# A hybrid state-space and attention network in fp32 on one core: the turned state-space steps listed anew, piece by piece, and the squares added on VectorE

## The chip, the cores and the metric

One core of a Trainium2 chip. The metric is device time in microseconds of one execution of the whole program (256 tokens through 4 layers). Shown are the median of three runs and, for the profile, one execution taken by the hardware profiler.

## The reference

Four layers of width 1024 on 256 tokens. Each layer is a half-weighted SwiGLU feed-forward (hidden width 2816), a mixer, and a second half-weighted feed-forward, each followed by a residual sum and a layer norm. The mixers are a Mamba-2 state-space mixer (layers 0 and 3), a forgetting attention (layer 1) and a block attention (layer 2). The change concerns the state-space mixer:

```python
zxbcdt = x @ w_in                                   # z 2048, x 2048, b 512, c 512, dt 32
xbc = silu(causal_conv4(xbc) + conv_b)
dt = softplus(dt + dt_bias); a = -exp(a_log)
decay = exp(segsum(dt * a))                         # per head, 256 x 256, lower triangle
y = ((c @ b.T) * decay) @ (x * dt) + x * d_skip     # 4 groups of 8 heads of 64
y = y * silu(z)
y = y * rsqrt(mean(y**2 over the 512 of a group) + eps) * norm_w
out = y @ w_out
```

## The kernel before, in words

All products run on TensorE (PE) in float32r, with each operand split in a high and a low part: `mm3` (L183) and `proj_T` (L269) issue three matmuls for one product. ACT makes the high part of a weight piece (`wh`, L156), DVE the low part (`wl`, L157). Weights stream from memory as pieces of 128x2048 fp32, 1 MB each, fetched by the SP queue (`fetch`, L159) two pieces ahead of use, with 3 raw and 5 split buffers.

The 256 tokens are two halves, t = 0 and t = 1, each a Python generator that takes one piece per step; the driver (L930 to L945) runs t = 1 two pieces behind t = 0. A state-space stage has 29 pieces in the order of `SSM_ORDER` (L44): X0 (4 pieces, not turned), Z0 (2, not turned), and then X1 to X3 (3 each), Z1 to Z3 (2 each) and the output pieces O0 to O3 (2 each), where the digit is the group. For X and Z of groups 1 to 3 the product is made once for both halves, turned (channels on the partitions), within t = 1; t = 0 has no work in these pieces. O pieces are done by each half for itself.

After a piece's product a list `post` names the steps that are issued: `at(i, step, ...)` appends a step to piece i. The steps of a group g are:

- `stage_T` (L493): ACT copies the turned product out of PSUM (L497), then the causal convolution (`conv`, L451: ACT L457, DVE L461) and its Silu (L464).
- `stage_e` (L531): the SP queue loads a row of cumulative sums broadcast over partitions, ACT makes four Relu (L544) and one Exp (L545), and for i = 1 one more Exp (L542). Tiles "mt", 5 buffers.
- `stage_back` (L502): three matmuls of b and c (L514), eight transposes (L521), DVE scales (L509, L524, L526).
- `stage_m` (L547) and `stage_y` (L552): DVE applies c b to the decays, PE makes y into a "gu" PSUM tile, DVE adds the skip (L570) into the tile Y.
- `stage_z` (L573): ACT's Silu of z (L575). `stage_g` (L577): DVE multiplies Y by it (L583, L589), ACT squares it (L592), POOL adds the squares of the two tiles (L593) and then the two halves of that (L594).
- `stage_r` (L597): PE sums over partitions with a column of ones (L601), DVE L603, POOL takes the power -1/2 (L605). `stage_n` (L607): PE broadcasts (L610), DVE scales Y (L615). `stage_a` (L617): Y is split into high and low parts for the O pieces.

PSUM has 8 banks: two each of "acc0" and "acc1", "gu" and "tp". Before the first output piece (less two) the turned products use the acc tiles, after that the "gu" tiles, since the output accumulators need all four (L679). The transposes and y use "tp" and "gu".

The list gives the program order. A scheduler then orders each engine's instructions by their readiness, with the program order as priority; `keep_in_program_order` pins an instruction behind what its engine was given before it (the matmuls of back and y are pinned).

Of the kernel before, what the change touches and what calls it, by code (L numbers as in the profile page):

```python
# [7 lines left out]
F32 = mybir.dt.float32  # L8
# [8 lines left out]
S = 256  # L17
# [9 lines left out]
N_GRP = 4  # L27
# [6 lines left out]
PF = 2  # L34
WB = 5
RB = 3

# [41 lines left out]
def build(tc, x, wst, ln_g, ln_b, sm_rows, sm_conv, fx_b, out, plan=None):  # L79
# [318 lines left out]
    def ssm_small(j):  # L398
        if j in ssms:
            return ssms[j]  # L400
        consts()
        s = St()
        s.rows = tmp(64, "rows", 1)
        tc.keep_in_program_order(nc.sync.dma_start(s.rows, bc(sm_rows[j:j + 1, :], 64)))
        s.conv = spool.tile([128, 24, 7], F32, name="conv", bufs=1)
        nc.sync.dma_start(s.conv, sm_conv[j])
        s.na = tmp(32, "na", 1)
        tc.keep_in_program_order(nc.scalar.activation(s.na, s.rows[:, 32:64], AF.Exp))
        nc.vector.tensor_scalar_mul(s.na, s.na, -1.0)
        s.xb, s.cv, s.xs, s.th, s.Y, s.cb, s.mt, s.d = {}, {}, {}, {}, {}, {}, {}, {}  # L410
        s.ahs = [{}, {}]
        ssms[j] = s
        return s

    def ssm(st, j):
# [77 lines left out]
        def stage_T(g, n):  # L493

            if n == 0:
                frame(g)
            nc.scalar.activation(s.xb[g][:, 2 * n:2 * n + 2, 3:3 + S],  # L497
                                 bank.pop(("X", g, n)).rearrange("p (a b) -> p a b", a=2), AF.Copy)
            if n:
                conv(g, 0 if n == 1 else 4, 2 * n + 2)  # L500

# [29 lines left out]
        def stage_e(g, qd, i):  # L531

            def tile_e():
                return spool.tile([128, 4, 128], F32, name="mt", bufs=5)
            e = tile_e()
            h0 = g * 8 + qd * 4
            row = s.d[i].cum[h0:h0 + 4, :].rearrange("h l -> (h l)").unsqueeze(0)
            nc.sync.dma_start(e.rearrange("p a b -> p (a b)"), row.to_broadcast([128, 512]))
            s.mt[g, qd, i] = e
            if i == 1:  # L540
                o = s.mt[g, qd, 2] = tile_e()
                nc.scalar.activation(o, e, AF.Exp)  # L542
            for h in range(4):
                nc.scalar.activation(e[:, h], e[:, h], AF.Relu, scale=-1.0, bias=s.d[i].cums[:, h0 + h:h0 + h + 1])  # L544
            nc.scalar.activation(e, e, AF.Exp, scale=-1.0)  # L545
# [25 lines left out]
                                               op0=ALU.mult, op1=ALU.add)  # L571

        def stage_z(g, n):  # L573
            th = s.th[g, n] = tmp(512, "nw" if g else "xD", 2)
            nc.scalar.activation(th, bank.pop(("Z", g, n)), AF.Silu)  # L575

        def stage_g(g):  # L577

            for n in range(2):
                Y = s.Y[g, n]  # L580
                if g:
                    th = s.th.pop((g, n)).rearrange("p (a b) -> p a b", a=2)
                    nc.vector.tensor_mul(Y, Y, th)  # L583
                else:
                    th = s.th.pop((0, n))
                    tp = transposes(th, 4).rearrange("p (n a b) -> p n a b", n=2, a=2)
                    for k in range(2):
                        Yk = s.Y[0, k][:, :, tok[n]]
                        nc.vector.tensor_mul(Yk, Yk, tp[:, k])  # L589
            sq = [tmp(512, "nw", 2) for n in range(2)]  # L590
            for n in range(2):
                nc.scalar.activation(sq[n], s.Y[g, n].rearrange("p a b -> p (a b)"), AF.Square)  # L592
            nc.gpsimd.tensor_add(sq[0], sq[0], sq[1])  # L593
            nc.gpsimd.tensor_add(sq[0][:, 0:S], sq[0][:, 0:S], sq[0][:, S:2 * S])  # L594
            s.sq = sq[0]

        def stage_r():  # L597

            ps = T()
            for i in range(2):  # L600
                nc.tensor.matmul(ps[:, i:i + 1], s.sq[:, tok[i]], K["cut"][:, 128:129], start=True, stop=True)  # L601
            ss = s.ss = small()
            nc.vector.tensor_scalar(ss[:, 0:2], ps[:, 0:2], 1.0 / 512, EPS, op0=ALU.mult, op1=ALU.add)  # L603
            for i in range(2):
                nc.gpsimd.tensor_tensor(ss[:, 2 + i:3 + i], ss[:, i:i + 1], mhalf, op=ALU.pow)  # L605

        def stage_n(g):  # L607
            ps = T()
            for i in range(2):
                nc.tensor.matmul(ps[:, tok[i]], s.ss[:, 2 + i:3 + i].to_broadcast([128, 128]), ident, start=True, stop=True)  # L610
            for n in range(2):
                for i in range(2):
                    w = s.conv[:, g * 6 + 2 * n + i]
# [22 lines left out]
        if t == 0:  # L636
            at(where["Z", 0, 1], stage_z, 0, 0)
        else:
            at(where["Z", 0, 1], stage_z, 0, 1)
# [24 lines left out]
        first_o = where["O", 0, 0]  # L664
        for i, (kind, g, n) in enumerate(pieces):
            if kind == "X" and g == 0:
                if n % 2 == 0:
                    ps = bank["b" if n == 0 else 0] = GA(int(n == 0))
            elif kind == "Z" and g == n == 0:
                ps = bank["Z", 0, t] = GA(1)  # L670
            w = yield
            if kind == "O":
                down(st, *s.ahs[t][g][n], w, g == 0 and n == 0, g == 3 and n == 1)
# [2 lines left out]
            elif kind == "Z" and g == 0:  # L676
                proj512(st, ps, n, w)
            elif t == 1:
                ps = bank[kind, g, n] = GA(int(kind == "Z")) if i < first_o - LAG else G()  # L679
                proj_T(ps, w)  # L680
            for f, a in post.get(i, ()):
                f(*a)
# [14 lines left out]
    def attn(st, kind, j):  # L697
# [62 lines left out]
        def stage_s(g):  # L760
# [18 lines left out]
            pt = [tmp(512, "mt", 5) for b in range(1 + t)]  # L779
# [21 lines left out]
        def att(g):  # L801

            pT = ps_.pop(g) if away(g) else []
            for p in () if away(g) else ps_.pop(g):
                tp = transposes(p, 4)
                e = tmp(512, "mt", 5)
                if t == 0:
                    nc.vector.tensor_copy(e, tp)
                else:
# [266 lines left out]
```

## Time and profile before

| | us |
|---|---|
| median of 3 runs (lowest, highest) | 2111.68 (2108.36, 2114.94) |
| the profiled execution, its own time | 2111.97 |
| its span, first to last instruction | 2110.1 |
| busy in the span: PE / weight loads / DVE / ACT / POOL | 2077.8 / 1759.7 / 1462.3 / 1169.3 / 527.4 |

The first state-space stage lies at about 193 to 385 us of the span, the second at about 1721 to 1913 us. PE is the matmul engine, PEld its weight loads, which run beside matmuls. A matmul is drawn longer than the distance to the next one, since matmuls are pipelined. "Idle before" with an arrow names what ended the wait.

### The profile page before, as it was taken

What the parts mean: (1) busy time and instruction counts of PE and PEld (TensorE: products, weight loads), DVE (VectorE), ACT (ScalarE), POOL (GpSimd) and SP (SyncE); (2) the same over time, 40 slices, a digit from 0 to 9 for tenths busy, and PEclk for the clock granted to TensorE, in tenths of its full rate; (3) what the DMA queues carried; (4) which work ended last, traced back from release to release, by engine and by line L of the source; (5) the groups of instructions that cost most, each with busy time, mean ns of one, the idle gap of its engine ahead of it and who ended that gap; (6) DMA issues with size and microseconds to landing.
All of it is one profiled execution on the core that took longest, in us unless ns stands there. A gap on an engine that the chain in (4) does not pass through costs nothing.

```text
span 2110.1 us, 31413 instructions
## 1 busy us (share of the span) xinstructions
PE 2077.8 (98%) x11034; PEld 1759.7 (83%) x11034; DVE 1462.3 (69%) x2912; ACT 1169.3 (55%) x2409; POOL 527.4 (25%) x937
## 2 busy tenths in 40 slices
PE   8999999999999999999999999999999999999998
PEld 7888988888888889788888889788888889888886
DVE  6557988765665676765675676755575589888565
ACT  6445998444544454545454455544545459984442
POOL 2331001233133313043233302033233310012331
PEclk9999999999999999999999999999999999999999
DMA  9766544677586665477676666376666765446762
GB/s 318 224 230 214 194 165 155 222 232 230 177 273 218 226 224 188 149 237 230 203 241 228 225 222 200 135 242 229 224 227 228 226 214 185 165 155 230 228 226 94
DMA packets 228493, 444.98 MB, mean 211 GB/s; under 512 B 21168, under 2 KB 21744, under 8 KB 228336
## 3 DMA queue, kind: packets, MB, share of 16 engines
q1 hardware_dynamic: 197616, 395.65, 55.4%
q0 software_dynamic: 30720, 47.34, 7.9%
q8 instruction: 86, 1.41, 0.3%
q14 instruction: 71, 0.58, 0.1%
HBM read 418.15 MB, written 24.76 MB: 210 GB/s over the span
## 4 chain that ended last, share of the span: by engine, by line
PE 87%; DVE 6%; ACT 4%; DMA 2%; issue 1%; POOL 0%; DVEq 0%; ACTq 0%; POOLq 0%
PE gu L184 15%; PE gu L187 15%; PE gu L188 15%; PE acc L184 9%; PE acc L187 9%; PE acc L188 9%; PE ga L276 2%; PE ga L278 2%; PE ga L277 2%; DVE wl L157 2%; PE tp L196 2%; ACT wh L156 1%; PE ga L184 1%; DVE cv L461 1%; PE ga L188 1%; PE ga L187 1%
## 5 line engine op out<-in xcount | busy, mean ns | idle before, releaser
L157 DVE TENSOR_TENSOR wl<-raw,wh 128x512 fp32r<-128x512 f32 (+1 forms) x1412 | 891.0, 682 | 348.0 <-ACT wh L156 346.5
L156 ACT ACTIVATE wh<-raw 128x512 fp32r<-128x512 f32 (+1 forms) x1412 | 779.3, 620 | 548.0 <-PE gu L188 217.0
L184 PE MATMUL gu<-wh,x 128*128 128x512 f32 x1408 | 548.8, 390 | 1.9 <-ACT wh L156 1.2
L188 PE MATMUL gu<-wh,x 128*128 128x512 f32 x1408 | 549.1, 390 | 0.0
L187 PE MATMUL gu<-wl,x 128*128 128x512 f32 x1408 | 548.8, 390 | 0.0
L300 POOL DMA_DIRECT2D aT<-turn x640 | 348.3, 551 | 517.5 <-issue 269.4
L184 PE MATMUL acc<-wh,ah 128*128 128x512 f32 x896 | 352.5, 395 | 4.8 <-ACT wh L156 4.5
L187 PE MATMUL acc<-wl,ah 128*128 128x512 f32 x896 | 352.6, 393 | 0.6 <-DVE wl L157 0.6
L188 PE MATMUL acc<-wh,al 128*128 128x512 f32 x896 | 351.5, 393 | 0.0
L184 PEld LDWEIGHTS gu<-wh,x 128*128 128x128 f32 x1408 | 264.8, 188 | 58.1 <-DVE t L326 1.7
L188 PEld LDWEIGHTS gu<-wh,x 128*128 128x128 f32 x1408 | 264.7, 188 | 55.4 <-DVE x L157 0.4
L187 PEld LDWEIGHTS gu<-wl,x 128*128 128x128 f32 x1408 | 264.7, 188 | 55.3 <-DVE wl L157 0.5
L324 ACT ACTIVATE t<-gu 128x256 f32<-128x256 f32 x176 | 67.4, 383 | 269.1 <-PE gu L188 248.5
L326 DVE TENSOR_TENSOR t<-t,gu 128x256 f32<-128x256 f32 x176 | 73.4, 417 | 191.6 <-ACT t L324 191.6
L184 PEld LDWEIGHTS acc<-wh,ah 128*128 128x128 f32 x896 | 168.5, 188 | 43.9 <-ACT wh L156 8.1
L187 PEld LDWEIGHTS acc<-wl,ah 128*128 128x128 f32 x896 | 168.8, 188 | 36.7 <-DVE wl L157 2.5
L188 PEld LDWEIGHTS acc<-wh,al 128*128 128x128 f32 x896 | 168.6, 188 | 35.3 <-DVE al L157 1.1
L276 PE MATMUL ga<-x,wh 128*128 128x256 f32 x608 | 174.2, 287 | 0.0
L278 PE MATMUL ga<-x,wl 128*128 128x256 f32 x608 | 174.0, 286 | 0.0
L277 PE MATMUL ga<-x,wh 128*128 128x256 f32 x608 | 173.5, 285 | 0.0
L296 POOL DMA_DIRECT2D turn<-tb x160 | 90.3, 565 | 298.4 <-DVE tb L294 277.4
L276 PEld LDWEIGHTS ga<-x,wh 128*128 128x128 f32 x608 | 117.0, 192 | 1.3 <-issue 0.7
(201 smaller groups left out, 2119.7 us busy)
## 6 DMA issues: line engine op xcount, KB each, us to landing
raw<-in_w_dram SPq DMA_DIRECT2D x354, 1024.0 KB, 5.6
turn<-tb POOLq DMA_DIRECT2D x160, 128.0 KB, 3.4
aT<-turn POOLq DMA_DIRECT2D x640, 32.0 KB, 4.1
mt<-cums SPq DMA_DIRECT2D x32, 256.0 KB, 5.6
gb<-in_ln_g_dram SPq DMA_DIRECT2D x12, 512.0 KB, 4.1
gb<-in_ln_b_dram SPq DMA_DIRECT2D x12, 512.0 KB, 5.3
turnp<-nw POOLq DMA_DIRECT2D x10, 256.0 KB, 3.7
t<-turnp POOLq DMA_DIRECT2D x40, 64.0 KB, 3.1
```

Source lines behind the costliest of these rows:

```text
L156: a = nc.scalar.activation(wh, raw, AF.Copy)
L157: return a, nc.vector.tensor_sub(wl, raw, wh.bitcast(F32))
L184: first = nc.tensor.matmul(o, xh, wh, start=start, stop=False)
L187: nc.tensor.matmul(o, xh, wl, start=False, stop=False)
L188: nc.tensor.matmul(o, xl, wh, start=False, stop=stop)
L276: nc.tensor.matmul(o, wh[:, sl], x4[:, 0:2, k], start=k == 0, stop=False, skip_group_check=True)
L277: nc.tensor.matmul(o, wh[:, sl], x4[:, 2:4, k], start=False, stop=False, skip_group_check=True)
L278: nc.tensor.matmul(o, wl[:, sl], x4[:, 0:2, k], start=False, stop=k == KT - 1, skip_group_check=True)
L296: nc.gpsimd.dma_start(dr, b.rearrange("p q k t -> p (q k t)"))
L300: nc.gpsimd.dma_start(aT[32 * q:32 * q + 32].rearrange("p i k t -> p i (k t)"), dv[q])
L324: nc.scalar.activation(sg, gu[:, :256], AF.Silu)
L326: nc.vector.tensor_mul(a, sg, gu[:, 256:])
```

## The change

It writes the steps of t = 1 as one table of pieces and steps, moves O0 ahead of X3 and Z2 behind X3 in the order of the pieces, lets DVE instead of POOL add the squares of the two tiles and PE the two halves, keeps the sums per group, moves both Silu of Z0 into t = 1, lets groups 1 to 3 write the squares over the gates, and changes two buffer counts. The steps of t = 0 that are not z stay.

```diff
-SSM_ORDER = ["X0", "Z0", "X1", "Z1", "X2", "Z2", "X3", "O0", "Z3", "O1", "O2", "O3"]
+MT = 6
+SSM_ORDER = ["X0", "Z0", "X1", "Z1", "X2", "O0", "X3", "Z2", "Z3", "O1", "O2", "O3"]
...
-        return tmp(32, "sm", 16)
+        return tmp(32, "sm", 10)
...
-                return spool.tile([128, 4, 128], F32, name="mt", bufs=5)
+                return spool.tile([128, 4, 128], F32, name="mt", bufs=MT)
...
-            th = s.th[g, n] = tmp(512, "nw" if g else "xD", 2)
-            nc.scalar.activation(th, bank.pop(("Z", g, n)), AF.Silu)
+            th = s.th[g, n] = tmp(512, "nw" if g % 2 else "xD", 2)
+            nc.scalar.activation(th, s.z.pop((g, n)), AF.Silu)
...
-            sq = [tmp(512, "nw", 2) for n in range(2)]
+            sq = [s.th.pop((g, n)) if g else tmp(512, "nw", 2) for n in range(2)]
             for n in range(2):
                 nc.scalar.activation(sq[n], s.Y[g, n].rearrange("p a b -> p (a b)"), AF.Square)
-            nc.gpsimd.tensor_add(sq[0], sq[0], sq[1])
-            nc.gpsimd.tensor_add(sq[0][:, 0:S], sq[0][:, 0:S], sq[0][:, S:2 * S])
-            s.sq = sq[0]
-        def stage_r():
+            nc.vector.tensor_add(sq[0], sq[0], sq[1])
+            s.sq[g] = sq[0]
+        def stage_r(g):
             ps = T()
             for i in range(2):
-                nc.tensor.matmul(ps[:, i:i + 1], s.sq[:, tok[i]], K["cut"][:, 128:129], start=True, stop=True)
-            ss = s.ss = small()
+                for k in range(2):
+                    nc.tensor.matmul(ps[:, i:i + 1], s.sq[g][:, k * S + i * 128:k * S + i * 128 + 128],
+                                     K["cut"][:, 128:129], start=k == 0, stop=k == 1)
+            ss = s.ss[g] = small()
...
-            split_at = (where["X", 2, 2],) * 2, (where["O", 0, 1],) * 2, (where["O", 2, 0] - 3, where["O", 1, 1])
-            for g, when in enumerate(split_at):
-                for i in range(2):
-                    at(when[i], stage_a, g, i)
-            for g in range(N_GRP):
-                b = where["X", g, 2 if g else 3]
-                for n in range(3 if g else 0):
-                    at(b - 2 + n, stage_T, g, n)
-                for n in range(2 if g else 0):
-                    at(where["Z", g, n], stage_z, g, n)
-                at(b, stage_e, g, 0, 1)
-                at(b + 1, stage_back, g)
-                at(b + 1, stage_e, g, 0, 0)
-                at(b + 1, stage_e, g, 1, 0)
-                at(b + 2, stage_m, g, 0)
-                at(b + 2, stage_y, g, 0)
-                at(b + 2, stage_e, g, 1, 1)
-                at(b + 3, stage_m, g, 1)
-                at(b + 3, stage_y, g, 1)
-                at(b + 4, stage_g, g)
-                at(b + 5, stage_r)
-                at(b + 6, stage_n, g)
-            at(where["O", 3, 0] - 3, stage_a, 3, 0)
-            at(where["O", 2, 1], stage_a, 3, 1)
+                    (3, [(e, 0, 0, 1)]),
+                    (4, [(back, 0), (e, 0, 0, 0), (e, 0, 1, 0)]),
+                    (5, [(m, 0, 0), (y, 0, 0), (e, 0, 1, 1)]),
+                    (6, [(m, 0, 1), (y, 0, 1), (T_, 1, 0), (z, 0, 0), (z, 0, 1)]),
+                    (7, [(T_, 1, 1), (gate, 0)]),
+                    (8, [(T_, 1, 2), (e, 1, 0, 1), (e, 1, 0, 0)]),
+                    (9, [(r, 0), (back, 1), (e, 1, 1, 0), (e, 1, 1, 1)]),
+                    (10, [(m, 1, 0), (y, 1, 0), (n_, 0)]),
+                    (11, [(m, 1, 1), (y, 1, 1), (T_, 2, 0), (z, 1, 0), (z, 1, 1), (a, 0, 0), (a, 0, 1)]),
+                    (12, [(T_, 2, 1), (gate, 1)]),
+                    (13, [(T_, 2, 2), (e, 2, 0, 1)]),
+                    (14, [(r, 1), (back, 2), (e, 2, 0, 0), (e, 2, 1, 0), (e, 2, 1, 1)]),
+                    (15, [(m, 2, 0), (y, 2, 0), (n_, 1)]),
+                    (16, [(m, 2, 1), (y, 2, 1), (T_, 3, 0), (e, 3, 0, 1), (e, 3, 0, 0)]),
+                    (17, [(e, 3, 1, 0), (e, 3, 1, 1), (T_, 3, 1)]),
+                    (18, [(T_, 3, 2), (a, 1, 0), (a, 1, 1)]),
+                    (19, [(z, 2, 0), (back, 3)]),
+                    (20, [(z, 2, 1), (m, 3, 0), (y, 3, 0), (gate, 2)]),
+                    (21, [(z, 3, 0), (m, 3, 1), (y, 3, 1), (r, 2)]),
+                    (22, [(z, 3, 1), (n_, 2), (a, 2, 0), (gate, 3)]),
+                    (23, [(r, 3)]),
+                    (24, [(a, 2, 1), (n_, 3), (a, 3, 0)]),
+                    (26, [(a, 3, 1)])):
```

With the new order, pieces 0 to 13 are X0, Z0, X1, Z1 and X2, 14 and 15 are O0, 16 to 18 X3, 19 to 22 Z2 and Z3, and 23 to 28 O1 to O3. Before, 14 and 15 were Z2, 19 and 20 O0. The two attention mixers take the sixth "mt" buffer as well.

## Rows read from the trace of the kernel before

**Rows 1.** Busy time in both state-space stages (193 to 385 and 1721 to 1913 us) and in 140 us within the first. After the stretch and its length: busy us and instructions of PE, PEld, DVE, ACT and POOL, the granted clock, the DMA share and GB/s.

```profile
193.00:385.00 192.00, 185.18 (x1346) 167.78 (x1345) 165.87 (x347) 159.88 (x310) 16.22 (x20) 0.99 0.54 182
1721.00:1913.00 192.00, 184.48 (x1345) 167.78 (x1344) 165.77 (x346) 160.06 (x310) 16.07 (x20) 0.99 0.53 181
220.00:360.00 140.00, 134.68 (x1087) 123.54 (x1086) 124.68 (x254) 129.96 (x252) 11.33 (x15) 1.00 0.53 174
```

**Rows 2.** Whom PE waited for in the first state-space stage, 193 to 385 us: us in total, times, longest.

```profile
PE tp L601 <- POOL nw L594: 3.3, 3, 1.5
PE acc L184 <- ACT wh L156: 2.2, 2, 1.8
PE tp L610 <- POOL sm L605: 0.7, 3, 0.3
PE acc L187 <- DVE wl L157: 0.3, 1, 0.3
```

**Rows 3.** The same in the second state-space stage, 1721 to 1913 us; a fourth row reads word for word as the last of rows 2 (0.3 us for DVE's L157).

```profile
PE tp L601 <- POOL nw L594: 4.2, 3, 2.0
PE acc L184 <- ACT wh L156: 2.3, 2, 1.8
PE tp L610 <- POOL sm L605: 0.5, 2, 0.3
```

**Rows 4.** PE in order of time from 366 us: start, length, engine, line, tiles, shape, and in brackets the idle time before and what ended it.

```profile
368.72 0.61 PE L601 MATMUL tp<-cut,nw 128*128 128x1 f32 x4 [1.50 <-POOL nw L594]
...
370.65 0.63 PE L187 MATMUL acc<-wl,ah 128*128 128x512 f32 x1
371.07 0.63 PE L188 MATMUL acc<-wh,al 128*128 128x512 f32 x1
...
373.84 0.39 PE L187 MATMUL acc<-wl,ah 128*128 128x512 f32 x1
374.06 0.39 PE L188 MATMUL acc<-wh,al 128*128 128x512 f32 x1
```

**Rows 5.** Two stretches of 20 us, one in each stage, with columns as in rows 1 (the granted clock stands after POOL).

```profile
360.00:380.00 20.00, 18.50 (x92) 15.38 (x91) 11.78 (x21) 9.22 (x19) 3.89 (x4) 0.91 0.44 163
1780.00:1800.00 20.00, 18.42 (x149) 18.29 (x151) 18.16 (x37) 19.08 (x34) 3.08 (x5) 0.91 0.31 106
```

**Rows 6.** POOL in order of time from 240 us.

```profile
250.37 1.43 POOL L593 TENSOR_TENSOR nw<-nw 128x512 f32<-128x512 f32 x1 [20.28 <-ACT nw L592]
251.88 0.79 POOL L594 TENSOR_TENSOR nw<-nw 128x256 f32<-128x256 f32 x1
```

**Rows 7.** DVE in order of time from 216 us, and after it one group of the table of lines of the whole program (busy us, mean ns of one, idle us before).

```profile
225.45 2.85 DVE L461 SCALAR_TENSOR_TENSOR cv<-xb,conv,cv 128x256 f32<-128x256 f32 x7
...
248.99 6.33 DVE L461 SCALAR_TENSOR_TENSOR cv<-xb,conv,cv 128x256 f32<-128x256 f32 x12
...
255.85 0.14 DVE L603 TENSOR_SCALAR sm<-tp 128x2 f32<-128x2 f32 x1
...
L583 DVE TENSOR_TENSOR t<-t,nw 128x512 f32<-128x512 f32 x12 | 8.3, 688 | 0.4
```

**Rows 8.** PE in order of time from 252 us.

```profile
252.72 0.60 PE L601 MATMUL tp<-cut,nw 128*128 128x1 f32 x4 [1.10 <-POOL nw L594]
253.19 0.36 PE L277 MATMUL ga<-x,wh 128*128 128x256 f32 x1
```

**Rows 9.** ACT's loads of function tables in the first state-space stage, by the line that wanted them: count, total us, mean ns. L464 is the convolution's Silu, L545 and L542 Exp, L575 z's Silu.

```profile
L464 ACT ACT_TABLE_LOAD x7 | 9.0, 1283 | 0.1
L545 ACT ACT_TABLE_LOAD x5 | 6.4, 1283 | 0.1
L575 ACT ACT_TABLE_LOAD x4 | 5.1, 1283 | 0.1
L542 ACT ACT_TABLE_LOAD x4 | 5.1, 1283 | 0.1
```

**Rows 10.** ACT in order of time from 298 us.

```profile
316.52 2.18 ACT L156 ACTIVATE wh<-raw 128x512 fp32r<-128x512 f32 x4
...
336.88 1.28 ACT L464 ACT_TABLE_LOAD   x1
...
340.22 1.28 ACT L545 ACT_TABLE_LOAD   x1
...
342.05 1.66 ACT L156 ACTIVATE wh<-raw 128x512 fp32r<-128x512 f32 x3
...
356.85 0.60 ACT L575 ACTIVATE nw<-gu 128x512 f32<-128x512 f32 x1
```

**Rows 11.** PE at the longest wait for a weight piece.

```profile
342.72 0.50 PE L184 MATMUL acc<-wh,ah 128*128 128x512 f32 x1 [1.82 <-ACT wh L156]
```

**Rows 12.** PE in order of time from 354.9 us: the first matmuls of a y (L563), the first of five output matmuls, and the first of the next turned piece.

```profile
354.92 0.44 PE L563 MATMUL gu<-mt,xdt 128*64 128x128 f32 x4
...
356.38 0.50 PE L187 MATMUL acc<-wl,ah 128*128 128x512 f32 x1
...
357.65 0.28 PE L276 MATMUL gu<-x,wh 128*128 128x256 f32 x1
```

**Rows 13.** The weight fetches of the whole program: count, KB each, median us from issue to landing.

```profile
raw<-in_w_dram SPq DMA_DIRECT2D x354, 1024.0 KB, 5.6
```

More of the change, by code (lines that the diff above doesn't have):

```diff
@@ L410, in ssm_small @@
         s.xb, s.cv, s.xs, s.th, s.Y, s.cb, s.mt, s.d = {}, {}, {}, {}, {}, {}, {}, {}
+        s.sq, s.ss, s.z = {}, {}, {}
         s.ahs = [{}, {}]
@@ L497, in stage_T @@
             nc.scalar.activation(s.xb[g][:, 2 * n:2 * n + 2, 3:3 + S],
-                                 bank.pop(("X", g, n)).rearrange("p (a b) -> p a b", a=2), AF.Copy)
+                                 bank.pop((g, n)).rearrange("p (a b) -> p a b", a=2), AF.Copy)
             if n:
@@ L573, in stage_z @@
         def stage_z(g, n):
-            th = s.th[g, n] = tmp(512, "nw" if g else "xD", 2)
-            nc.scalar.activation(th, bank.pop(("Z", g, n)), AF.Silu)
+            th = s.th[g, n] = tmp(512, "nw" if g % 2 else "xD", 2)
+            nc.scalar.activation(th, s.z.pop((g, n)), AF.Silu)
         def stage_g(g):
             for n in range(2):
-                Y = s.Y[g, n]
+                Y, th = s.Y[g, n], s.th[g, n]
                 if g:
-                    th = s.th.pop((g, n)).rearrange("p (a b) -> p a b", a=2)
-                    nc.vector.tensor_mul(Y, Y, th)
+                    nc.vector.tensor_mul(Y, Y, th.rearrange("p (a b) -> p a b", a=2))
                 else:
-                    th = s.th.pop((0, n))
                     tp = transposes(th, 4).rearrange("p (n a b) -> p n a b", n=2, a=2)
@@ L609, in stage_n @@
             for i in range(2):
-                nc.tensor.matmul(ps[:, tok[i]], s.ss[:, 2 + i:3 + i].to_broadcast([128, 128]), ident, start=True, stop=True)
+                nc.tensor.matmul(ps[:, tok[i]], s.ss[g][:, 2 + i:3 + i].to_broadcast([128, 128]), ident,
+                                 start=True, stop=True)
             for n in range(2):
@@ L635, in ssm @@
         at(where["X", 0, 3] + 1 - t, stage_cum)
[L636 to L639, printed above, removed]
-            split_at = (where["X", 2, 2],) * 2, (where["O", 0, 1],) * 2, (where["O", 2, 0] - 3, where["O", 1, 1])
-            for g, when in enumerate(split_at):
-                for i in range(2):
-                    at(when[i], stage_a, g, i)
-            for g in range(N_GRP):
-                b = where["X", g, 2 if g else 3]
-                for n in range(3 if g else 0):
-                    at(b - 2 + n, stage_T, g, n)
-                for n in range(2 if g else 0):
-                    at(where["Z", g, n], stage_z, g, n)
-                at(b, stage_e, g, 0, 1)
-                at(b + 1, stage_back, g)
-                at(b + 1, stage_e, g, 0, 0)
-                at(b + 1, stage_e, g, 1, 0)
-                at(b + 2, stage_m, g, 0)
-                at(b + 2, stage_y, g, 0)
-                at(b + 2, stage_e, g, 1, 1)
-                at(b + 3, stage_m, g, 1)
-                at(b + 3, stage_y, g, 1)
-                at(b + 4, stage_g, g)
-                at(b + 5, stage_r)
-                at(b + 6, stage_n, g)
-            at(where["O", 3, 0] - 3, stage_a, 3, 0)
-            at(where["O", 2, 1], stage_a, 3, 1)
@@ new lines, in ssm @@
+        if t == 1:
+            e, back, m, y, T_, z, gate = stage_e, stage_back, stage_m, stage_y, stage_T, stage_z, stage_g
+            r, n_, a = stage_r, stage_n, stage_a
+            for i, steps in (
+                    (3, [(e, 0, 0, 1)]),
[21 more added lines that the diff above has]
+                    (26, [(a, 3, 1)])):
+                for step in steps:
+                    at(i, *step)
@@ L669, in ssm @@
             elif kind == "Z" and g == n == 0:
-                ps = bank["Z", 0, t] = GA(1)
+                ps = s.z[0, t] = GA(1)
             w = yield
@@ L678, in ssm @@
             elif t == 1:
-                ps = bank[kind, g, n] = GA(int(kind == "Z")) if i < first_o - LAG else G()
+                ps = GA(int(kind == "Z")) if i < first_o - LAG else G()
+                (s.z if kind == "Z" else bank)[g, n] = ps
                 proj_T(ps, w)
@@ L778, in stage_s @@
                         tc.keep_in_program_order(ins)
-            pt = [tmp(512, "mt", 5) for b in range(1 + t)]
+            pt = [tmp(512, "mt", MT) for b in range(1 + t)]
             for b in range(2):
@@ L805, in att @@
                 tp = transposes(p, 4)
-                e = tmp(512, "mt", 5)
+                e = tmp(512, "mt", MT)
                 if t == 0:
```

## The prediction

> **What bounds the kernel now.** TensorE does. I read the busy shares first, then one table of stretches, then who PE waited for, then single instructions. Of the span of 2110.1 us it is busy 2077.8, so it idles 32.3 us. In the two state-space stages, 192 us each, it is busy 185.18 and 184.48 us and idles 6.8 and 7.5, 14.3 us in all [rows 1]. Elsewhere the change touches only two buffer counts, so this is the pool from which it can draw. In the same stages ACT is busy 129.96 of 140 us and DVE 124.68 [rows 1], so three engines run almost evenly loaded there, and a late instruction on ACT or DVE reaches PE.
>
> PE's waits by their end [rows 2, 3]: for L594, the second POOL addition ahead of the sums of squares, 3.3 + 4.2 us in 6 waits; for a weight piece that ACT or DVE had not yet split (L156, L157), 2.2 + 0.3 + 2.3 + 0.3 us in 6 visible waits; for the POOL power L605 ahead of the norm, 0.7 + 0.5 us in 5. That is 13.8 of the 14.3 us.
>
> These idle times are shorter than the loss. A 128x512 matmul is drawn 0.39 us long, but its follower starts 0.22 to 0.23 us after it (373.84 to 374.06 [rows 4]), so idle time counts from some 0.16 us too late: the wait shown as 1.50 us made L601 1.66 us late. I add 0.16 us per wait: POOL additions 7.5 + 6 x 0.16 = **8.5 us**, weight pieces 5.1 + 6 x 0.16 = **6.1 us**, powers 1.2 + 5 x 0.16 = **2.0 us**.
>
> One more loss hangs on the longest of these. After these 1.66 us the matmuls start 0.42 us apart instead of 0.23 for some 3 us (370.65 to 371.07, against 373.84 to 374.06) [rows 4], and the granted clock of that stretch is 0.91, as it is once in the second stage [rows 5]: 9% of 20 us missing is 3.6 us at the lower of the two levels (1.2 instead of 2.4 GHz). Seven matmuls with 0.2 us extra and the edges make 1.6 us, twice **3.2 us**. In the first stage it follows the wait for L594 within 2 us [rows 4].
>
> **The change, part by part.**
>
> *Sum of squares.* Today the squares go to POOL, 1.43 + 0.79 us with a gap, and TensorE's L601 is queued behind [rows 6]. The change makes one 128x512 addition on DVE (nearest row: the 128x512 gate product L583, 0.69 us [rows 7]) and lets TensorE sum the two halves: four listed matmuls for two. The row counts each listed one twice (x4 for two), and from the first to what follows takes 252.72 to 253.19, 0.47 us [rows 8]. So 8 groups cost 8 x 0.47 = **3.8 us** more on PE, surely on the path. The wait of 8.5 us should go for two reasons: the chain gets 2.4 - 0.7 = 1.7 us shorter, and L601 is listed two pieces behind its gate instead of one for groups 0 and 1, while the gate of group 2 has long had its Y. Behind the last piece the listing is as before, and there 1.66 - 1.7 leaves about nothing.
>
> What queues behind the addition on DVE: the convolution L461. It gains. Seven convolution steps took 2.85 us, 0.40 each; twelve took 6.33 us where POOL's additions ran beside them (248.99 to 255.32 against 250.37 to 252.67), 1.5 us more than 12 x 0.40 [rows 6, 7]. So DVE gives 0.6 us and gets 1.5 us back in a group.
>
> The Trainium skill ("SBUF — State Buffer", Who interferes with whom) says that a VectorE instruction with two SBUF inputs and a GpSimd one that reads SBUF exclude each other for a whole instruction. By that rule 2.2 us, not 1.5, would come back in a group; the trace agrees that the two slow each other, with 1.5 us. It would make my second rival below less likely still, and leaves the sum alone.
>
> *Exponentials and gates listed together.* By the old list ACT's function changes between the Silu set and the Exp set 18 times from piece 3 on (counted by hand), and the trace has 20 loads at these four lines in one stage [rows 9]. The new list has 6 changes: Exp at 3, Silu at 6, Exp at 8, Silu at 11, Exp at 13, Silu at 17. The order on the engine need not be the listed one: at 336.88 Silu was loaded and at 340.22 Exp again [rows 10]. The new list has three places of that kind (after T of groups 1, 2, 3), so I take 8 to 12. At 1.28 us a load [rows 9] 8 to 12 of them fewer free ACT for 10 to 15 us in a stage. This does not shorten PE's path by itself. It is worth the weight waits: the longest, 1.82 us, ends on a split of 342.05 that stood behind the two loads just named, and PE starts 0.67 us behind it [rows 10, 11]. Gain **6.1 us**, bounds 0 and 6.1.
>
> *Output pieces O0 ahead of X3, Z2 after it.* The last group's chain (turn, convolution, Silu, back, y) had only O0 and early O1 pieces beside it, and the 1.82 us of [rows 11] is PE running ahead into an unsplit O1. Now the pieces Z2 and Z3 stand there, whose weights come four steps ahead of use. That helps the same 6.1 us, so it is not counted again.
>
> *Powers.* L603 read the sums of 252.72 only at 255.85, behind the convolution block [rows 7, 8]. In the new list the norm follows at least a piece, and mostly also a y, behind its sum: the **2.0 us** go.
>
> *What it adds.* (a) From X2's second piece on, the turned pieces use the two "gu" buffers, which y and back use too. A piece can start only when ACT has copied or gated the one that holds its buffer. That was so once before: Z3's second piece started at 357.65, just behind its buffer's Silu at 356.85 + 0.60, and five other matmuls filled the gap [rows 10, 12]. Now there are four such places in a stage (X3's first to second piece, Z2 to Z2, Z2 to Z3, Z3 to Z3), each covered by a y of about 1.4 us (354.92 to 356.38, 1.46) or a back; a free ACT needs 0.6 us. Bounds 0 and 2.6 us per place (four splits 2.18, a load 1.28, the evacuation 0.60, less 1.46 [rows 9, 10, 12]); I take 0.5, nearest to the row that was filled: 8 x 0.5 = **4.0 us**. (b) n of group 2 and its split now stand in the step just ahead of O2 of the first token half (before, n stood three steps ahead of that split). Bounds in a stage 0 and 1.6 us (two L615, a split of ACT and one of DVE, all 128x256; nearest row the 0.40 us of a convolution step [rows 7]); another O1 piece can go ahead, so I take 0.5 us, in all **1.0 us**. (c) A sixth "mt" buffer, 10 instead of 16 "sm", z in one place, and the SP queue's row loads in another order past the weight loads: 0, hidden by the two to four steps between load and use; without that cover each late load would cost up to its 5.6 us [rows 13].
>
> **The sum** against the profiled execution (span 2110.1, 1.9 us around it, 2111.97, 0.3 above the median 2111.68): - 8.5 - 6.1 - 2.0 - 3.2 + 3.8 + 4.0 + 1.0 = -11.0, so **2101.0 us**. Bounds of this case: without (a) and (b) 2096, and 2094 if also half of the 3.8 us hides, the added sums' weights loading beside other matmuls; with 1.5 us in each place of (a) 2109.
>
> **Rivals.**
> - *Buffers bind (slower).* Each of the eight places of (a) waits its bound of 2.6 us, 20.8 us, and the clock then falls as before, so 3.2 us are not gained: -16.6 + 3.8 + 20.8 + 1.0 = +9.0, **2121**. From 1.5 us per place on ((16.6 - 3.8 - 1.0) / 8) the gain of the rest is gone. For it: between X3's pieces nothing else is listed for PE. Against: ACT has 10 to 15 us more room, and no load of a table is due among the Z pieces. The Trainium skill ("Perfetto Trace Analysis", Optimization Strategy) says that the same gap coming again and again on the engine that should be saturated can mean too few buffers; no such gap stands in this trace. Chance 0.10.
> - *The addition is late on DVE.* L601 waits for DVE as it did for POOL, since DVE runs blocks of convolution of up to 6.33 us [rows 7]: 8.5 and 3.2 are not gained, -8.1 + 8.8 = +0.7, **2113**. Chance 0.12.
> - *The change doesn't do what it says on ACT.* The engine's order follows readiness, the loads stay near 20 and the weight waits of 6.1 us with them: **2107**. Chance 0.12.
>
> **How the numbers follow.** The forecast has 0.66, its own range 2094 to 2109. A measurement of this kernel tells about 0.3%, 6.3 us, from no change, so the line is 2105.4. Nearly all of the forecast and a quarter of the third rival lie below it: faster 0.68. Within: the second rival, most of the third, the forecast's upper end: 0.22. Slower: the buffer rival, 0.10. The range 2093 to 2113 takes in the forecast and the rivals at 2107 and 2113, and leaves out the slow rival and a tail.
>
> **What would show it.** Right: no wait of PE for POOL's L593 and L594 (gone) and under 1 us for the new addition; table loads at the four lines from 20 to between 8 and 12 in a stage; PE idle 3 to 5 us in each stage instead of 7; granted clock 1.00 all through; eight L601 groups with x8. Wrong: PE waits at "gu" tiles for L497 or L575; L601 waiting for DVE; loads still near 20; or more idle time in the attention layers, whose "mt" buffers change too.

## The result, and the profile after

| | before | after |
|---|---|---|
| median of 4 runs each, us | 2111.05 (2108.36 to 2114.94) | 2142.38 (2141.14 to 2143.64) |
| ratio, 95% interval | | 1.0147 (1.0129 to 1.0165) |
| profiled execution, span, us | 2110.1 | 2139.4 |
| first state-space layer, norm to norm, us | 199.60 | 213.10 |
| second, us | 199.95 | 211.58 |
| attention layer with the forgetting gate, norm to norm, us | 119.6 | 122.8 |

The forecast was 2101.0, range 2093 to 2113; the change costs 31 us. The layer norms tell where: DVE's aggregation (the instruction that makes a norm's mean and variance) of the first token half stands once ahead of each mixer and once behind it. In the kernel before it starts at 187.18, 386.78, 1715.11 and 1915.06 us. After (DVE in order of time):

```profile
187.27 0.20 DVE L230 BATCH_NORM_AGGREGATE mv<-stats 128x2 f32<-128x12 f32 x1
400.37 0.21 DVE L230 BATCH_NORM_AGGREGATE mv<-stats 128x2 f32<-128x12 f32 x1
...
1731.81 0.20 DVE L230 BATCH_NORM_AGGREGATE mv<-stats 128x2 f32<-128x12 f32 x1
1943.39 0.21 DVE L230 BATCH_NORM_AGGREGATE mv<-stats 128x2 f32<-128x12 f32 x1
```

The two differences, summed, I call the **stage sum**: 399.55 us before, 424.68 after, +25.1 of the 29.3 in span. The attention layer, whose code the change touches in buffer counts alone, gives 3.1 more; it is dealt with at the end. One profile, that of e10 below, is of a disturbed execution of 7297.6 us and has no stage sum.

Busy time in the two stages and in four stretches of 20 us in the first (columns as in [rows 1]):

```profile
193.24:392.00 198.76, 182.14 (x1332) 167.43 (x1331) 155.07 (x340) 155.26 (x303) 8.87 (x12) 0.97 0.49 169
1737.80:1936.00 198.20, 182.29 (x1336) 167.64 (x1335) 156.11 (x342) 155.15 (x303) 8.80 (x12) 0.97 0.50 171
260.00:280.00 20.00, 12.01 (x113) 11.42 (x111) 16.54 (x35) 19.88 (x38) 1.14 (x3) 0.97 0.30 110
280.00:300.00 20.00, 19.59 (x131) 17.55 (x132) 15.26 (x32) 18.96 (x36) 0.00 (x0) 0.86 0.47 161
300.00:320.00 20.00, 13.48 (x90) 11.46 (x88) 14.57 (x30) 18.49 (x36) 1.19 (x3) 0.91 0.41 155
320.00:340.00 20.00, 20.00 (x166) 19.70 (x167) 10.62 (x23) 15.57 (x33) 0.00 (x0) 0.92 0.51 162
```

PE idles 16.6 and 15.9 us where it idled 6.8 and 7.5 [rows 1]: +18.2. The missing clock of the four stretches is 0.03 + 0.14 + 0.09 + 0.08, 6.8 us at full speed, against 1.8 before [rows 5]; some of it falls on idle time, so it adds 0 to 5.0 in a stage. With the 3.8 us forecast for the added sums this makes 22 to 32, around the 25.1 measured. Norm to norm, where PE idles no longer than in these windows, its busy time rises by 3.7 and 3.2 us (192.78 to 196.48 and 192.43 to 195.67): idle and busy time together are the 25.1.

Whom PE waited for in the first stage, 193 to 392 us (us, times, longest), against [rows 2]:

```profile
PE gu L565 <- DVE mt L552: 8.2, 3, 5.3
PE acc L185 <- ACT ah L157: 6.3, 1, 6.3
PE tp L516 <- ACT cv L466: 1.2, 1, 1.2
PE acc L185 <- ACT wh L157: 0.8, 1, 0.8
```

The three causes of before are gone or small: no wait for an addition, none for a power, 0.8 us for a weight piece instead of 2.5. In their place stand a y (L565) that waits for m's products and O0's first matmul, which waits for its split. PE at both, and ACT ahead of the second:

```profile
270.19 0.28 PE L279 MATMUL ga<-x,wl 128*128 128x256 f32 x1
272.59 0.66 PE L565 MATMUL gu<-mt,xdt 128*64 128x128 f32 x8 [2.12 <-DVE mt L552]
...
280.41 0.79 PE L185 MATMUL acc<-wh,ah 128*128 128x512 f32 x1 [6.29 <-ACT ah L157]
...
311.14 0.68 PE L612 MATMUL tp<-ident,sm 128*128 128x128 f32 x4
317.12 1.12 PE L565 MATMUL gu<-mt,xdt 128*64 128x128 f32 x8 [5.30 <-DVE mt L552]
```

```profile
273.44 3.73 ACT L157 ACTIVATE wh<-raw 128x512 fp32r<-128x512 f32 x7
277.08 0.57 ACT L499 ACTIVATE xb<-ga 128x512 f32<-128x512 f32 x1
277.67 1.28 ACT L578 ACT_TABLE_LOAD   x1
278.97 1.08 ACT L578 ACTIVATE nw<-ga 128x512 f32<-128x512 f32 x2
279.94 1.33 ACT L157 ACTIVATE ah<-t 128x256 fp32r<-128x256 f32 x4
```

The split of group 0 (279.94) stands behind seven weight splits, the turned copy, a table load and two Silu: the change lists it last in step 11, behind the turned copy and both Silu. PE meanwhile has nothing: X2's next piece is listed behind the output piece.

ACT's table loads at the four lines of [rows 9] (L466, L547, L544, L578 now) are 18 instead of 20:

```profile
L466 ACT ACT_TABLE_LOAD x9 | 11.5, 1283 | 0.1
L547 ACT ACT_TABLE_LOAD x5 | 6.4, 1283 | 0.1
L544 ACT ACT_TABLE_LOAD x3 | 3.8, 1283 | 0.1
...
L578 ACT ACT_TABLE_LOAD x1 | 1.3, 1283 | 0.0
```

### The profile page after: what moved, and what is told of

It is laid out like the page before. It is cut to its first block, busy times and chain, and to the rows that moved or that the text cites. A ratio compares the mean times of both kernels' runs of the same rounds, so it can differ in the third digit from the quotient of the medians.

```text
span 2139.4 us, 31460 instructions
## 1 busy us (share of the span) xinstructions
PE 2086.7 (98%) x11066; PEld 1771.2 (83%) x11066; DVE 1452.2 (68%) x2920; ACT 1164.6 (54%) x2405; POOL 512.7 (24%) x921
## 4 chain that ended last, share of the span: by engine, by line
PE 86%; ACT 6%; DVE 4%; DMA 2%; issue 1%; SPq 0%; DVEq 0%; POOL 0%; ACTq 0%; POOLq 0%
PE gu L185 15%; PE gu L188 15%; PE gu L189 15%; PE acc L185 9%; PE acc L189 9%; PE acc L188 9%; DVE wl L158 2%; PE tp L197 2%; ACT wh L157 2%; PE ga L279 1%; PE ga L277 1%; PE ga L278 1%; PE gu L565 1%; PE ga L185 1%; PE ga L189 1%; PE ga L188 1%
## 5 line engine op out<-in xcount | busy, mean ns | idle before, releaser
L157 ACT ACTIVATE wh<-raw 128x512 fp32r<-128x512 f32 (+1 forms) x1412 | 778.7, 620 | 568.3 <-PE gu L189 216.5
L277 PE MATMUL ga<-x,wh 128*128 128x256 f32 x448 | 128.6, 287 | 0.0
L279 PE MATMUL ga<-x,wl 128*128 128x256 f32 x448 | 127.9, 285 | 0.0
L278 PE MATMUL ga<-x,wh 128*128 128x256 f32 x448 | 127.6, 285 | 0.0
L234 POOL TENSOR_TENSOR rstd<-ve,mhalf 128x1 f32<-128x1 f32 x24 | 22.6, 944 | 324.0 <-DVE ve L232 324.0
```

Of the source, the lines that this page charges most:

```text
L157: a = nc.scalar.activation(wh, raw, AF.Copy)
L277: nc.tensor.matmul(o, wh[:, sl], x4[:, 0:2, k], start=k == 0, stop=False, skip_group_check=True)
L278: nc.tensor.matmul(o, wh[:, sl], x4[:, 2:4, k], start=False, stop=False, skip_group_check=True)
L279: nc.tensor.matmul(o, wl[:, sl], x4[:, 0:2, k], start=False, stop=k == KT - 1, skip_group_check=True)
```

## The experiments

The theories at first: (1) the new order of the pieces costs the time, (2) the new list of exponentials and gates does, (3) the sums on VectorE do. Ratios are against the kernel before on the same chip, where its median was 2111.1 to 2113.3; the stage sum is of the one profiled execution, which can lie off the median (e4: 2126.1, e14: 2121.7). A recorded ratio and that of the two medians differ by up to 0.18% (e7: 0.9953 against 2106.1 / 2112.2 = 0.9971), so differences of under 4 us between runs are not read.

| run | median, us | ratio, 95% interval | stage sum |
|---|---|---|---|
| before | 2112 | | 399.6 |
| after | 2142.4 | 1.0147 (1.0129 to 1.0165) | 424.7 |
| e1 sums only | 2107.4 | 0.9979 (0.9969 to 0.9988) | 391.8 |
| e2 order only | 2127.1 | 1.0071 (1.0055 to 1.0088) | 414.2 |
| e3 change, old order | 2116.4 | 1.0017 (1.0005 to 1.0030) | 401.1 |
| e4 change, two moves | 2131.8 | 1.0091 (1.0071 to 1.0112) | 413.5 |
| e5 gu rule | 2117.3 | 1.0017 (1.0004 to 1.0029) | 404.7 |
| e6 order, late y | 2108.5 | 0.9971 (0.9956 to 0.9986) | 396.1 |
| e7 sums, buffers | 2106.1 | 0.9953 (0.9936 to 0.9969) | 389.5 |
| e8 the same, early exponentials | 2117.4 | 1.0012 (0.9999 to 1.0025) | 399.8 |
| e9 change, split early | 2127.3 | 1.0061 (1.0047 to 1.0075) | 410.6 |
| e10 change, three moves | 2132.5 | 1.0087 (1.0071 to 1.0103) | none |
| e11 the same, old exponentials | 2119.6 | 1.0037 (1.0024 to 1.0050) | 407.2 |
| e12 order, late y, sums, buffers | 2102.1 | 0.9940 (0.9927 to 0.9953) | 384.3 |
| e13 as e11, norm early | 2111.3 | 0.9993 (0.9982 to 1.0005) | 397.8 |
| e14 as e11, Silu early | 2114.1 | 1.0010 (0.9997 to 1.0024) | 402.6 |
| e15 as e11, both | 2110.5 | 0.9995 (0.9984 to 1.0006) | 395.7 |
| e16 change, squares on POOL | 2142.8 | 1.0146 (1.0127 to 1.0164) | 430.0 |
| e17 as e15, gate buffers | 2111.7 | 0.9996 (0.9985 to 1.0007) | 395.4 |
| e18 as e17, order within a step | 2101.7 | 0.9946 (0.9926 to 0.9966) | 385.5 |

**e1, sums only.**

```diff
-            nc.gpsimd.tensor_add(sq[0], sq[0], sq[1])
-            nc.gpsimd.tensor_add(sq[0][:, 0:S], sq[0][:, 0:S], sq[0][:, S:2 * S])
+            nc.vector.tensor_add(sq[0], sq[0], sq[1])
...
+                for k in range(2):
+                    nc.tensor.matmul(ps[:, i:i + 1], s.sq[:, k * S + i * 128:...], ..., start=k == 0, stop=k == 1)
```

> The kernel before with the sum of squares of the change alone: one addition on VectorE, four listed matmuls for two; order of the pieces and list of steps as before. The terms of the prediction give 2112 - 8.5 (waits for POOL's addition) - 3.2 (half clock) + 3.8 (more matmuls) = 2104. Theory 1 (the order of the pieces costs the time) and theory 2 (the list of exponentials and gates costs it) both expect 2102 to 2106. Theory 3 (the squares on VectorE cost it, the addition standing behind the convolution there and the sums on TensorE waiting for it) expects 2120 or more.

2107.4: faster by 5.0 us in the medians, 1.4 us above the range, and the stage sum is 7.7 us lower where the terms gave 8.5 + 3.2 - 3.8 = 7.9. No sum waits for DVE. Theory 3 falls.

**e2, order only.** `SSM_ORDER` of the change in the kernel before; split of group 0 at 11, of group 1 at 18, gate, sum and norm of group 2 at 20 to 22.

> The kernel before with the order of the pieces alone: O0 ahead of X3, Z2 behind it; only the steps that the order forces are moved (splits of group 0 to piece 11, of group 1 to 18, gate, sum and norm of group 2 to 20 to 22). Exponentials, gates and POOL's additions stay as they were listed. Theory 1 (O0 asks for the split of group 0 before ACT has it, and leaves TensorE nothing beside the chain of group 2): 2130 to 2145, with a wait of over 3 us at O0's first matmul and one at group 2's first y. Theory 2 (the list): 2105 to 2118, no such waits.

2127.1, stage sum +14.6: half of the loss, and 3 us under the range of theory 1. No wait at O0, but 5.2 us at group 1's second y and 5.4 at group 2's first. So the wait for the split in the changed kernel comes from its list (here the split is listed first in step 11), not from the order.

**e3, old order.** The changed kernel with the old `SSM_ORDER`, Silu of group 2 at 16.

> The changed kernel with the old order of the pieces: Z2 at 14 and 15, O0 at 19 and 20; the two Silu of group 2 are listed at 16, all else as in the changed list. Theory 1: the waits at O0 and at group 2's first y go, 2100 to 2115. Theory 2 (the list makes exponentials and products late whatever the order): 2130 to 2145, with waits of TensorE for m's product at groups 1 and 2.

2116.4, 1.4 above the range of theory 1. The order takes most of the loss with it; but e1 was 2107.4, so some 9 us stay with the list or the buffer counts.

**e4, two moves.**

```diff
-(10, [(m, 1, 0), (y, 1, 0), (n_, 0)]),
-(11, [(m, 1, 1), (y, 1, 1), (T_, 2, 0), (z, 1, 0), (z, 1, 1), (a, 0, 0), (a, 0, 1)]),
+(10, [(n_, 0), (a, 0, 0), (m, 1, 0), (y, 1, 0)]),
+(11, [(m, 1, 1), (y, 1, 1), (a, 0, 1), (T_, 2, 0), (z, 1, 0), (z, 1, 1)]),
...
-(15, [(m, 2, 0), (y, 2, 0), (n_, 1)]),
+(15, [(n_, 1)]),          # m, y of group 2 now at 16 and 17
```

> The changed kernel with two moves in its list and nothing else: norm and first split of group 0 lead step 10, its second split leads step 11; m and y of group 2 go one piece later, 16 and 17, so that X3's first piece can run beside the exponentials. Theory 1, in the form that the two stalls are waits for steps that are listed too late or too early for their piece: the 6.5 us at O0 and the 5.5 us at group 2's first y go from both stages with the half clock behind them, 2 x (12 + 6.8) = 38 less half of it given back, 2115 to 2125. Theory 2: a few us at most, 2135 to 2142.

2131.8: 10.5 us back, less than the 17 to 27 expected. The wait at O0 is gone; 3.7 us at group 1's first y and 3.5 at group 2's stay.

**e5, the bank rule alone.** Turned pieces from 12 on take the gu banks, order and list as before: `i < 12` for `i < first_o - LAG`.

> The kernel before, its order and list untouched; only the PSUM banks differ: the turned pieces from number 12 on (X2's second) take the two gu banks, as the new order makes them, instead of the accumulators from number 17 on. Theory 1a (the early O0 costs because it takes the accumulators from X2, so that X2's pieces can no longer run ahead of group 1's second y): the 5.4 us stall of the run with the order alone appears at that y (about 273 to 278 of the first stage) and the time is 2117 to 2124. Theory 1b (the short output pieces next to the chain are the cost, the banks nothing): 2108 to 2114 and no stall over 1 us there.

The stall appears where theory 1a put it. PE, and DVE around it:

```profile
274.71 0.28 PE L278 MATMUL ga<-x,wl 128*128 128x256 f32 x1
280.17 0.69 PE L563 MATMUL gu<-mt,xdt 128*64 128x128 f32 x4 [5.18 <-issue]
```

```profile
273.78 0.87 DVE L570 SCALAR_TENSOR_TENSOR t<-cv,conv,gu 128x256 f32<-128x256 f32 x2
...
279.38 0.69 DVE L550 TENSOR_TENSOR mt<-mt,t 128x512 f32<-128x512 f32 x1
```

The first y's bank is read out by 274.65 (273.78 + 0.87), so X2's second piece could start then. It does not: on PE's list it stands behind the second y, whose product (279.38) is late. The view names no releaser ("issue") for these 5.18 us; that the y waited for this product is read from its end at 280.07, 0.10 us ahead of the y. In the kernel before that y starts no earlier (278.99), but X2's pieces, in the accumulators, run ahead of it. The time is +5 (stage sum +5.1), below the 10.4 of the two stalls: the weight waits of [rows 2, 3] are gone here, and POOL's additions hold PE 2.7 and 2.6 us instead of 3.3 and 4.2.

**e6, order with late y.**

```diff
-                at(b + 2, stage_m, g, 0)          # and stage_y
+                at(b + 2 + int(g == 2), stage_m, g, 0)
...
-                at(b + 3, stage_m, g, 1)          # and stage_y
+                at(b + 3 + int(g in (1, 2)), stage_m, g, 1)
```

> The kernel before with the new order of the pieces, as in the run with the order alone, and three steps listed one piece later: second product and y of group 1 (12), both products and y of group 2 (16, 17). A piece of X2 and of X3 then stands ahead of the y that waits. Theory 1c (the stalls are TensorE standing at a y although a ready piece is listed behind it): both stalls of 5.4 us shrink below 2 us and the time is 2108 to 2116. Theory 1b (the chain of group 2 is simply too long for what work is left beside it): the stalls move to the next instruction of the chain and the time stays at 2122 to 2128.

2108.5, 18.6 us below e2 (stage sum -18.1), and faster than before. PE now starts X2's second piece as the first y's bank comes free:

```profile
270.99 0.39 PE L563 MATMUL gu<-mt,xe 128*64 128x128 f32 x4
...
272.48 0.28 PE L276 MATMUL gu<-x,wh 128*128 128x256 f32 x1
```

Theory 1c holds, 1b falls: the order is good; what cost in e2 was that three y were listed ahead of the piece that should cover them.

**e7, sums and buffers.** e1 with 10 sm and 6 mt buffers.

> The kernel before with the sums of the change and its two buffer counts (six mt for five, ten sm for sixteen), order and list as before. With the old order of the pieces the changed kernel measured 2116, the sums alone 2107; this tells which part holds the 9 us between them. If the fewer sm buffers hold up the chain of dt and so the first decays: 2114 to 2118. If it is the list of exponentials and gates: 2105 to 2109.

2106.1: the buffer counts cost nothing, the list holds the 9 us of e3.

**e8, early exponentials.** e7 with `stage_e(g, 1, 1)` of groups 1 to 3 one piece earlier.

> As the run before this, and one step more: the last exponentials of groups 1 to 3 are listed one piece earlier, with the others of their group, which six mt buffers allow. If late exponentials hold the wait of 2.06 us for a weight piece at the first output piece O1: that wait goes, 2100 to 2105. If ACT only shifts its other work by it: 2105 to 2110. If more exponentials in a row make the weight pieces late elsewhere: 2110 to 2118.

2117.4, +11 for three exponential steps moved one piece: the range of the third outcome, but not its mechanism, since PE waits 1.2 us for weight pieces in the first stage, less than the 2.4 of e7. PE there, where e7 has no wait at these lines:

```profile
336.45 0.94 PE L514 MATMUL tp<-cv 128*128 128x128 f32 x6 [1.96 <-ACT cv L464]
...
342.00 0.89 PE L563 MATMUL gu<-mt,xdt 128*64 128x128 f32 x8 [2.97 <-DVE mt L550]
```

The chain is not late: this Silu ends 149.4 us behind the layer's first aggregation, against 150.2 in e7. What PE lacks is other work. In e7 output matmuls start up to 337.78, just ahead of L514, and again from 339.64 to the y at 346.68; in e8 the last starts at 334.10, and between the transposes (338.43) and the y at 342.00 there are none. Why PE's order came out so is not shown.

**e9, split early.** The first half of e4 alone.

> The changed kernel with one move: norm and first split of group 0 lead step 10, its second split leads step 11 (the first half of the run with two moves). If the wait of 6.5 us at O0's first matmul is a price of its own: it goes in both stages with the half clock behind it (6.5 + 3.4 each), some of it comes back at the next y: 2127 to 2133, about what the two moves gave together. If O0 then only waits for another chain (second y of group 1, exponentials): 2138 to 2143.

2127.3, 15.1 below the changed kernel. The late y of group 2 in e4 thus cost 4.5 there by the medians, though the intervals of the two ratios overlap a little.

**e10, three moves.** e4 with m and y (1, 1) at 12.

> The changed kernel with the two moves (2132) and a third: second product and y of group 1 at 12 instead of 11, behind X2's second piece. By theory 1c (TensorE stands at a y with a ready piece listed behind it) the stall of 3.8 us at group 1 goes too: 2120 to 2126. If the early exponentials make the chain late whatever stands before it: 2128 to 2134.

2132.5: no gain over e4, theory 1c's number (2120 to 2126) missed.

**e11, old exponentials.** e10 with the exponentials of groups 1 to 3 at 8, 9, 9, 10; 13, 14, 14, 15; 18, 19, 19, 20.

> As the run before this, with the exponentials of groups 1 to 3 listed at the pieces of the kernel before (one piece apart instead of together); Silu, gates and norms stay as the change lists them. In the old order the new list cost 10 us (2116 against 2106) and exponentials one piece earlier cost 11 (2117 against 2106), so the theory that exponentials listed together push ACT's splits and convolution back expects 2104 to 2112. If Silu and gates hold the cost: as the run before this.

2119.6, 12.9 below e10: the exponentials are a cost, of the size of e3 and e8. But 2104 to 2112 was expected, so 8 us or more lie elsewhere.

**e12, all that gained.** e6 with the sums and buffer counts of e7.

> All parts that were seen to gain, on the kernel before: new order with the three late steps (2108.5), sums on VectorE and the two buffer counts (together 6 us less than before): 2099 to 2105 if they add, since the waits for POOL's additions (1.40, 1.26, 0.62, 0.62 us) are still there in the run with the late steps. If they draw on the same idle time: 2105 to 2109. If the exponentials and gates had to be listed anew for the new order: over 2109.

2102.1. They add, and this beats both kernels; it is 17.5 us below e11, which has the same order of pieces, sums and counts of sm and mt buffers. Waits of PE in its first stage (190 to 385 us) come down to one row:

```profile
PE gu L276 <- DVE t L570: 1.5, 1, 1.5
```

**e13 to e15, norm and Silu.** e11 with sums and norms of groups 0 and 1 at 8, 9, 13, 14 and the splits of group 0 at 11 (e13); with Silu of group 0 at 5 and of group 1 at 9 and 10 (e14); with both (e15).

> As the run with three moves and the old exponentials (2119.6), with sums and norms of groups 0 and 1 one piece earlier, as in the kernel before, and both splits of group 0 at 11. If O0's wait of 2.9 us for its split (273 of the first stage) comes from the late norm: that wait goes in both stages, 2110 to 2115. If it comes from ACT being full there: as before this move, 2117 to 2122.

> As the run with three moves and the old exponentials (2119.6), with the Silu of groups 0 and 1 listed behind their own pieces, as in the kernel before, instead of two together at 6 and at 11. If grouping the Silu costs ACT's time just ahead of O0 and makes the gates late: 2105 to 2113, with more table loads than 45. If it costs nothing: 2117 to 2122.

> Both moves of the two runs before this. Only the buffers of gates and squares are then left between this and the kernel that measured 2102. If list alone holds the 17 us: 2101 to 2106. If the buffers hold part of it: 2108 to 2116.

2111.3, 2114.1 (1 us above its range) and 2110.5. Each takes O0's wait of 2.7 us away, and together they give no more than e13 alone; perhaps both free the same moment on ACT and DVE, which is not shown. About 8 us above e12 stay.

**e16, squares on POOL.** The changed kernel with POOL's two additions and two listed sums.

> The changed kernel with the sum of squares as before: two additions on POOL, two listed matmuls. Alone the sums gained 4.5 us. If they gain the same here: 2145 to 2149. If the other waits of the changed kernel (exponentials, splits) hide POOL's addition, and only the added matmuls count: 2137 to 2142.

2142.8 against 2142.4, between the two ranges: by the medians the sums on VectorE are worth nothing inside the changed kernel. The stage sums say 5.3 us (430.0 to 424.7), but the attention layer took 2.9 us more in the one profile than in the other. I leave the size open.

**e17 and e18, the last 8 us.** e17 is e15 with Silu results and squares in the buffers of before. e18 is e17 with sum, norm, gate and splits of the older group ahead of the younger group's steps within a step (at 9 the Silu of group 1 also goes behind the norm of group 0, at 22 the gate of group 3 ahead of group 2's split):

```diff
-(12, [(m, 1, 1), (y, 1, 1), (T_, 2, 1), (gate, 1)]),
+(12, [(m, 1, 1), (y, 1, 1), (gate, 1), (T_, 2, 1)]),
...
-(18, [(T_, 3, 2), (e, 3, 0, 1), (a, 1, 0), (a, 1, 1)]),
+(18, [(a, 1, 0), (a, 1, 1), (T_, 3, 2), (e, 3, 0, 1)]),
```

and in the same way at 8, 9, 13, 20, 21, 22 and 24.

> As the run with norm and Silu early (2110.5), with the buffers of the Silu results and of the squares as in the kernel before (Silu results of groups 1 to 3 in nw, squares in nw of their own). If these buffers hold the remaining 8 us: 2101 to 2105. If not, the small differences of order within a step hold it: 2108 to 2113.

> As the run with the gate buffers put back (2111.7), with the order within a step as in the kernel before: sum, norm, gate and splits of the older group ahead of the turned copy, products and y of the younger one (steps 8, 9, 12, 13, 18, 20, 21, 22, 24). If the order within a step decides which of two ready instructions ACT and DVE take first, and so holds the last 8 us: 2101 to 2105. If not: 2109 to 2113, and the difference stays open.

2111.7 and 2101.7: the buffers nothing, the order within a step 10 us. Waits of PE in the first state-space stage of e17, then of e18:

```profile
PE gu L277 <- DVE t L572: 3.4, 1, 3.4
PE tp L516 <- ACT cv L466: 2.1, 1, 2.1
```

```profile
PE gu L277 <- DVE t L572: 1.6, 1, 1.6
PE tp L436 <- ACT dah L157: 0.7, 1, 0.7
```

The same steps in the same pieces: only their order within a piece has changed, and the wait for the convolution's Silu is gone. ACT also loads a table 20 times a layer instead of 22. That the order works through which of two ready instructions ACT and DVE take first is the reading of it; no swap was run alone. With it the two ways meet: e12, built up from the kernel before, and e18, built down from the change, are 2102.1 and 2101.7.

## Why the prediction was wrong

**The step that failed** is the one that cost next to nothing in it: the new list. "This does not shorten PE's path by itself", said of the exponentials, and "so it is not counted again", said of O0 ahead of X3, took a moved step for free as long as it had pieces between listing and use. It set gains against the list (6.1 us of weight waits, 2.0 of powers) and, as a cost, only the 1.0 us of (b). Between e18 and the changed kernel nothing differs but positions in the list, apart from the buffers of Silu results and squares, which e17 shows to cost nothing, and that is 2101.7 to 2142.4, 385.5 to 424.7 in stage sum. Going up, by medians: order within the steps 10 us, norm and Silu one piece later 8, exponentials together 13, the y moves back to the change's list -5, norm and split of group 0 late, the split behind Silu and turned copy, 15. The parts hold for this order of undoing: a late y gained 18.6 with the list of before (e6) and loses here.

**The sums** came out right in total: -8.5 - 3.2 + 3.8 = -7.9, measured -7.7 in the stage sum of e1 (5.0 by the medians). That close an agreement is partly luck. The price of one was high: from the first sum to what follows takes 0.80 us in the changed kernel (260.45 to 261.25), 0.33 more than in [rows 8], not 0.47; eight of them make 2.6, not 3.8. Against that, the clock came back in one stage only: from 1855 to 1875 us of e1 it is 0.91, behind a weight wait of 1.82 us, so about half of the 3.2 stayed.

```profile
260.45 0.95 PE L602 MATMUL tp<-cut,nw 128*128 128x1 f32 x8
261.25 0.36 PE L277 MATMUL ga<-x,wh 128*128 128x256 f32 x1
```

DVE gained as said: with POOL's additions gone, eight convolution steps take 3.25 us, 0.41 each, in e1, against 0.53 in the block of twelve of [rows 7]:

```profile
253.01 3.25 DVE L461 SCALAR_TENSOR_TENSOR cv<-xb,conv,cv 128x256 f32<-128x256 f32 x8
```

The rule of the Trainium skill ("SBUF — State Buffer", Who interferes with whom) agrees with that trace; the runs do not tell its whole-instruction form from a partial one.

**The weight waits** of 6.1 us go with the new order, if each y has its cover: e12 is 5.2 us below e7 in stage sum. All gains together, -15.2 (e12), stand against -8.5 - 6.1 - 2.0 - 3.2 + 3.8 = -16.0. The pool was read rightly, with errors inside it that cancel, as in the sums; the changed kernel did not draw on it.

**Term (a), the gu banks,** named the right resource and the wrong place and price: X3's and Z's pieces, with a y as cover. In e5 it is X2's second piece, and the y is not the cover but stands ahead of the piece on PE's list: 5.2 us each time, not 0.5. So the rival "buffers bind" had the right sign; its mechanism, a wait for ACT's evacuation, is 2.3 us in e4 and absent in the list of waits after. Where the stalls are gone, a bank does hold PE, and it is DVE that frees it: a turned piece waits until DVE has read a y out, 1.5 us in the first stage of e12 and 3.4 in e17, in the lines shown there. Term (b), 1.0 us, shows no wait after.

**The rival on table loads** was true in its fact (18 of 20 stay, where 8 to 12 were forecast), but the number of loads does not go with the time: counted over all lines, a state-space layer has 16 loads in e9 (2127), 20 in the changed kernel (2142) and in e12 (2102), 24 in e15 (2110). Loads were the wrong thing to count. **The rival on DVE's addition** is false: no sum waits for DVE, after or in e1. **Buffer counts**, costed at 0, cost 0 (e7).

**Open:** which of the swaps within the steps carries the 10 us; why moving group 2's y later gains with the old exponentials (e6) and loses with the new (e4 against e9); the worth of the sums inside the changed kernel (e16).

## What to carry to other kernels

Where one list feeds several in-order engines, price each position in it: ask for every waiting instruction which ready piece stands ahead of it on its engine, and for every engine whether the older group's step is listed ahead of the younger's. Moving an output piece forward also moves its PSUM banks, so look at which pieces lose the right to run ahead. Do one part of a change at a time: here parts worth 10 us were hidden under list positions that cost 40.

## What the runs showed of the hardware

A layer that was not meant to change varies by 7 us. The attention layer takes 118.3 to 125.5 us in the 19 profiles, and with it varies PE's wait for a transfer through memory (biases from fbias): at most 1.0 us in every profile where the layer is under 121 us, 1.2 to 3.7 in every longer one. None in e3 (118.3), then after (122.8) and e14 (125.5):

```profile
PE gu L775 <- DMA biases<-fbias: 2.3, 1, 2.3
```

```profile
797.02 0.58 PE L780 MATMUL gu<-biases,sel 64*128 64x256 f32 x1 [3.68 <-DMA biases<-fbias]
```

The granted clock of that layer is 1.00 in e3, 0.99 after and 0.97 in e14, so some of the time falls to the lower of the two levels behind the wait (0.50 from 797 to 803 us in e14). The sixth "mt" buffer is not it, since e3 has that too. With one profile for each kernel the runs do not tell scatter from an effect of what stands ahead of the layer. Seven us in one layer are as much as many single steps here; sums over the stages that a change touches tell more than the whole.
